# The first six expert matrices of a mixture of experts, loaded as halves into a pool that is then opened again

## The chip, the cores and the metric

The kernel runs on one core of one Trainium2 chip, as one program and one launch. The metric is the time of one execution on the device, in microseconds (us). TensorE is called PE below, VectorE DVE, ScalarE ACT, GpSimd POOL, and SyncE SP. SP issues every DMA of this kernel in the order of its own queue. Sizes of loads are in KB and MiB of 1024; rates are in GB/s of 10^9.

## The reference, cut to what matters

Two transformer blocks over 256 tokens of width 1024, all in fp32. The first block is a gated feed-forward layer, a recurrent mixer and a second gated feed-forward layer. The second block is an attention, a spatial gate, an output projection, and this mixture of experts, on which the change bears:

```python
for g in range(N_GROUPS):      # 4 groups of 8 experts, each expert 1024 x 512, 1024 x 512, 512 x 1024
    h = jax.nn.silu(jnp.einsum('nd,edf->nef', xt, w_gate[g])) * jnp.einsum('nd,edf->nef', xt, w_up[g])
    out = out + jnp.einsum('nef,efd->nd', h * combine[:, g, :, None], w_down[g])
```

Each token uses two experts of one group, but all 32 experts get tokens, so all 96 matrices of 2 MiB have to come out of HBM once: 192 MiB.

## The kernel before

The program runs through the first block, then through attention, gate and router of the second, and then through the experts. All weights ahead of the experts stream through SP into `wr` tiles of 1 MiB (line 118); ACT and DVE split each into a high part `whi` and a low part `wlo` for PE.

**The experts** run in 16 rounds `r`, two experts `e` = 0, 1 a round. A round needs three pairs of matrices `k`: gate (0), up (1), down (2). PE takes the pairs in the order (0,0), (0,1), (1,0), (1,1), (0,2), (2,0), (2,1), (1,2), (3,0) and so on, written (r,k): the down step of a round comes after gate and up of the next. `gate_up` (matmuls on line 1321) walks over j = 0..7 and takes e = 0 and e = 1 in turn at each j, so it reads the first half of both matrices at j = 0..3 and the second half of both at j = 4..7. In (0,0) the second half of `gather` stands between j = 3 and j = 4. `down` has its matmuls on line 1344. The matmuls and the small steps between them stand in an order written out by hand.

**Where the matrices lie.** A matrix is a tile `mw` of 16 KB on each of 128 partitions. There are 11 buffers. Six are the pool `mw1`, opened on the left side of SBUF at the end of the first block, so that its loads can start while attention still runs. Five are `mw2`, opened on the right side when attention is over and its buffers `wraw`, `whl`, `xgp` are given back. The matrices are numbered n = 0..95 in the order of use, and n takes buffer n mod 11: n = 0..5 are (0,0), (0,1), (1,0) in `mw1`, n = 6..10 lie in `mw2`, and n = 11, the second matrix of (2,0), is the first that goes back into a buffer of `mw1`, that of n = 0. It has one more place: its first half goes into `hx`, the 8 KB in which attention kept its result `h`, as soon as `h` is no longer needed.

```python
first = hx.tile([128, 2048], F32, name="hx")[:, :] if n_loads[0] == MW else None
t = whole_tile()
w.append([t[:, 0:2048] if first is None else first, t[:, 2048:4096]])
```

**What orders the loads.** Every load is issued by SP on line 1158. A load waits on SP until the last reader of what lay in its place is done, and the loads behind it in SP's queue wait with it. Up to the end of attention a scheduler decides how the loads of `wr` and of `mw` stand in that queue. Pools are opened with `reuse_waits="tile"`. The pool `mt2`, with the working tiles of the experts (`mxg`, `ms`, `hT`, `y`, ...), lies on the left in the place of attention's buffers.

Of the kernel before, what the change touches and what calls it, by code (L numbers as in the profile page):

```python
# [9 lines left out]
F32 = mybir.dt.float32  # L10
# [21 lines left out]
MW1 = 6  # L32
# [12 lines left out]
CUTS = ((0, 4096), (0, 2048, 4096), (0, 1024, 2048, 3072, 4096), (0, 1024, 2048, 3072, 3584, 4096))  # L45
# [28 lines left out]
def body(nc, tc, ap, dbg=None, stop=None):  # L74
    dbg = dbg or {}
    ctx = ExitStack()
# [6 lines left out]
    def pool(stack, name, bufs=1, space=None, side=None):  # L83
        kw = {"space": space} if space is not None else {}
        if side:
            kw["side"] = side
        return stack.enter_context(tc.tile_pool(name=name, bufs=bufs, reuse_waits="tile", **kw))
# [4 lines left out]
    with ctx:  # L92
# [87 lines left out]
        for q in range(4):  # L180
            r = slice(32 * q, 32 * q + 32)
# [43 lines left out]
        for q in range(4):  # L225
            r = slice(32 * q, 32 * q + 32)
# [136 lines left out]
        with ExitStack() as st:  # L363
            mp = pool(st, "mp")
            mt = pool(st, "mt", 2)
# [5 lines left out]
            parts = mp.tile([128, 2, 1024], F32R, name="parts")  # L371
# [72 lines left out]
            for base, src, dst, n in ((0, tw, sg, 0), (32, wa[32:64], ta, 4)):  # L444
                for h in range(2):
                    hs = slice(2 * h, 2 * h + 2)
                    ps = psR.tile([128, 2, T], F32, name="r")
                    for i in range(2):
                        p = 2 * h + i
                        TE.matmul(ps[:, i], lor[base:base + 32, p * 128:(p + 1) * 128], src, start=True, stop=True)  # L450
                    for i in range(2):
                        p = 2 * h + i
# [94 lines left out]
            for b in range(2):  # L547
                ms = [(i, c, 8 * i + 4 * b + c) for i in range(2) for c in range(4)]
                ps = psR.tile([128, 2, 4, C], F32, name="r")
                for i, c, m in ms:  # L550
                    for q in range(4):
                        r = slice(32 * q, 32 * q + 32)
# [3 lines left out]
                for i, c, m in ms:  # L556
                    for q in range(4):
                        r = slice(32 * q, 32 * q + 32)
                        TE.matmul(ps[r, i, c], NT[r, m], Yo[r, m], start=True, stop=True)
                for q in range(4):  # L560
                    r = slice(32 * q, 32 * q + 32)
# [38 lines left out]
            for s in range(2):  # L600
                r = sides[s]
# [14 lines left out]
            for c in range(NCH):  # L616
# [7 lines left out]
                if c < NCH - 1:  # L624
# [4 lines left out]
                    for s in range(2):  # L629
                        r = sides[s]  # L630
# [36 lines left out]
            for p in range(4):  # L667
                lerped(rr[:, p])
                for s in range(2):
                    r = sides[s]  # L670
# [158 lines left out]
            V.reciprocal(t[:, 1], t[:, 0])  # L829
            return t[:, 1]  # L830

        mw1 = pool(ctx, "mw1", MW1)
        hx = pool(ctx, "hx")
        hst = ctx.enter_context(ExitStack())
        hres = pool(hst, "hres")
        h = hx.tile([128, 2048], F32, name="hx").rearrange("p (a n) -> p a n", a=2)
# [6 lines left out]
        with ExitStack() as st:  # L843
# [134 lines left out]
            for i in range(4):  # L978
                q, k = following
# [154 lines left out]
        MW = MW1 + MW2  # L1134
        mw2 = [pool(ctx, f"mw2{i}", 1, side="right") for i in range(MW2)]
        rt = pool(ctx, "rt", side="right")
        n_loads = [0]

        def whole_tile():
            n = n_loads[0] % MW  # L1140
            p = mw1 if n < MW1 else mw2[n - MW1]
            n_loads[0] += 1
            return p.tile([128, 4096], F32, name="mw")

        def load(r, k):

            fine = 1 + k if r == 15 else int((r, k) == (14, 2))
            w, parts = [], []
            for e in range(2):
                first = hx.tile([128, 2048], F32, name="hx")[:, :] if n_loads[0] == MW else None  # L1150
                t = whole_tile()
                w.append([t[:, 0:2048] if first is None else first, t[:, 2048:4096]])
                cuts = CUTS[fine if first is None else 1]
                for s0, s1 in zip(cuts, cuts[1:]):
                    dst = t[:, s0:s1] if first is None or s0 else first
                    parts.append((s0, e, dst, ap["wm"][2 * r + e, k, :, s0:s1]))
            for s0, e, dst, src in sorted(parts, key=lambda x: x[:2]) if fine else parts:
                nc.sync.dma_start(dst, src)
            return w

        hnh = rt.tile([128, 2, D], F32R, name="hnh")
# [16 lines left out]
        with ExitStack() as st:  # L1178
# [15 lines left out]
            def small(name, k, n=None):  # L1194
                return rp.tile([128, k] + ([n] if n else []), F32, name=name)
# [51 lines left out]
            ex, w = small("ex", 8, 8), small("w", 6, 8)  # L1247
# [21 lines left out]


        with ExitStack() as st:
            mt = pool(st, "mt2", 1)
            psG = pool(st, "psG", 2, PSUM)
            psX = pool(st, "psX", 2, PSUM)
            def gather(g, steps=range(4), xg=None):
# [36 lines left out]
            def gate_up(r, k, mid=None):  # L1312

                w = load(r, k)
                ps = psG.tile([128, 512], F32, name="g")
                for j in range(NJ):
                    if mid and j == 4:
                        mid()
                    for e in range(2):
                        c = r % 2 * 128 + 64 * e  # L1320
                        TE.matmul(ps[64 * e:64 * e + 64], xg[:, j, c:c + 64],  # L1321
                                  w[e][j // 4][:, (j % 4) * 512:(j % 4) * 512 + 512], start=j == 0, stop=j == NJ - 1)
                return ps
# [11 lines left out]
            def down(r, hT, between=None):  # L1335

                wd = load(r, 2)
                pd = [psG.tile([128, 512], F32, name="g") for f in range(2)]
                ys = hx.tile([128, 2048], F32R, name="hx").rearrange("p (f n c) -> p f n c", n=2, f=2) if r == 15 else None
# [79 lines left out]
            tc.keep_in_program_order(S.preload_act_table_set("sqrt_and_others"))  # L1419


        fin = [mw1.tile([128, 4096], F32, name="mw") for n in range(2)]
        gfin, hsq, out = fin[0][:, 0:D], fin[1][:, 0:D], fin[1][:, 2048:4096].rearrange("p (a n) -> p a n", a=2)
        rowvec(gfin, "gfin")

# [23 lines left out]
        with tc.If(most > SLOT), ExitStack() as st:  # L1449
# [8 lines left out]
            with tc.For_i(0, NE, 1) as e:  # L1458
                w = []
# [7 lines left out]
                for n, src in enumerate((rk, comb)):  # L1467
                    m = ov.tile([128, 2, NE], F32, name="om")
# [135 lines left out]
```

## Time and profile before

| | |
|---|---|
| median of three runs | 1136.05 us (1135.2 to 1138.19) |
| the profiled execution's own time | 1135.7 us |
| its span, first to last instruction | 1134.0 us |
| around the span (launch, end) | 1.7 us |
| PE busy | 1079.0 us, 95% of the span |
| DVE, ACT, POOL busy | 538.7, 405.9, 139.5 us |
| moved by DMA | 304.69 MB, mean 269 GB/s |
| mean granted TensorE clock | 0.982 |

Busy time of PE is modelled from pipelined matmuls, so 95% does not say that PE sets the time of every stage. Shares over the whole span mix the first 680 us, where the weights move at some 180 GB/s, with the experts, where they move at 427 GB/s. The stages have to be read apart. The profiled execution is 0.35 us under the median of the three runs.

### The profile page before, as it was taken

What the parts mean: (1) busy time and instruction counts of PE and PEld (TensorE: products, weight loads), DVE (VectorE), ACT (ScalarE), POOL (GpSimd) and SP (SyncE); (2) the same over time, 40 slices, a digit from 0 to 9 for tenths busy, and PEclk for the clock granted to TensorE, in tenths of its full rate; (3) what the DMA queues carried; (4) which work ended last, traced back from release to release, by engine and by line L of the source; (5) the groups of instructions that cost most, each with busy time, mean ns of one, the idle gap of its engine ahead of it and who ended that gap; (6) DMA issues with size and microseconds to landing.
All of it is one profiled execution on the core that took longest, in us unless ns stands there. A gap on an engine that the chain in (4) does not pass through costs nothing.

```text
span 1134.0 us, 18469 instructions
## 1 busy us (share of the span) xinstructions
PE 1079.0 (95%) x7762; PEld 795.9 (70%) x7762; DVE 538.7 (48%) x966; ACT 405.9 (36%) x677; POOL 139.5 (12%) x139
## 2 busy tenths in 40 slices
PE   7999999868998999999999989999999999999996
PEld 6999999868788999999997864444344344534432
DVE  6766666799568766657655761211112121101112
ACT  5544454633544644445465631111011111101102
POOL 5000000663343200001134020000000000000000
PEclk9999999988998999999999999999999999999998
DMA  7655555422114555545677487999999999999994
GB/s 246 212 179 180 182 185 185 149 75 76 39 55 160 201 186 186 178 162 185 249 306 297 149 316 286 427 427 427 426 427 426 427 429 426 425 427 429 422 414 166
DMA packets 33319, 304.69 MB, mean 269 GB/s; under 512 B 4016, under 2 KB 4272, under 8 KB 9168
## 3 DMA queue, kind: packets, MB, share of 16 engines
q1 hardware_dynamic: 33232, 303.46, 67.8%
q8 instruction: 63, 1.03, 0.4%
q14 instruction: 24, 0.20, 0.1%
HBM read 302.40 MB, written 1.05 MB: 268 GB/s over the span
## 4 chain that ended last, share of the span: by engine, by line
PE 75%; DMA 14%; DVE 6%; ACT 2%; issue 1%; POOL 1%; SPq 0%; ACTq 0%; DVEq 0%; POOLq 0%
PE g L1321 14%; DMA mw<-wm 13%; PE gu L270 11%; PE gu L271 11%; PE gu L269 11%; PE g L1344 7%; PE u L269 3%; PE u L271 2%; PE u L270 2%; PE x L1286 2%; DVE wlo L261 1%; PE z L1375 1%; PE f L1375 1%; DMA wr<-w 1%; PE f L1006 1%
## 5 line engine op out<-in xcount | busy, mean ns | idle before, releaser
L261 DVE TENSOR_TENSOR wlo<-wr,whi 128x1024 fp32r<-128x1024 f32 (+3 forms) x182 | 202.7, 1119 | 93.9 <-ACT whi L260 92.8
L260 ACT CAST whi<-wr 128x1024 fp32r<-128x1024 f32 (+3 forms) x200 | 182.0, 918 | 168.0 <-PE gu L270 66.8
L1321 PE MATMUL g<-mw,mxg 128*64 128x512 f32 x1016 | 231.0, 595 | 1.2 <-DMA mw<-wm 1.2
L269 PE MATMUL gu<-xgh,whi 128*128 128x256 f32 x704 | 201.9, 287 | 6.8 <-ACT whi L260 6.8
L271 PE MATMUL gu<-xgh,wlo 128*128 128x256 f32 x704 | 201.4, 286 | 0.7 <-DVE wlo L261 0.7
L270 PE MATMUL gu<-xgl,whi 128*128 128x256 f32 x704 | 201.3, 286 | 0.5 <-DVE xgl L283 0.5
L1321 PEld LDWEIGHTS g<-mw,mxg 128*64 128x64 f32 x1016 | 76.0, 137 | 136.8 <-issue 129.3
L269 PEld LDWEIGHTS gu<-xgh,whi 128*128 128x128 f32 x704 | 137.0, 195 | 7.2 <-ACT whi L260 7.1
L271 PEld LDWEIGHTS gu<-xgh,wlo 128*128 128x128 f32 x704 | 136.9, 194 | 1.2 <-DVE wlo L261 1.2
L270 PEld LDWEIGHTS gu<-xgl,whi 128*128 128x128 f32 x704 | 137.0, 195 | 1.1 <-DVE xgl L283 1.0
L1344 PE MATMUL g<-mw,hT 128*64 128x512 f32 x512 | 121.1, 603 | 6.2 <-DMA mw<-wm 6.2
L269 PE MATMUL gu<-hh,whi 128*128 128x256 f32 x352 | 98.6, 280 | 0.0
L271 PE MATMUL gu<-hh,wlo 128*128 128x256 f32 x352 | 98.6, 280 | 0.0
L270 PE MATMUL gu<-hl,whi 128*128 128x256 f32 x352 | 98.0, 279 | 0.0
L1344 PEld LDWEIGHTS g<-mw,hT 128*64 128x64 f32 x512 | 39.9, 138 | 73.9 <-issue 59.1
L1350 ACT ACTIVATE y<-g,cs 128x512 fp32r<-128x512 f32 x30 | 20.6, 687 | 181.1 <-PE g L1344 120.5
L1351 DVE SCALAR_TENSOR_TENSOR y<-g,cs,y 128x512 fp32r<-128x512 f32 x30 | 22.5, 751 | 122.9 <-ACT y L1350 122.9
L269 PE MATMUL u<-xgh,whi 128*128 128x256 f32 x224 | 66.7, 298 | 1.7 <-DVE lb L434 1.2
L270 PE MATMUL u<-xgl,whi 128*128 128x256 f32 x224 | 65.6, 293 | 0.5 <-DVE xgl L283 0.5
L269 PEld LDWEIGHTS gu<-hh,whi 128*128 128x128 f32 x352 | 66.1, 188 | 0.0
L271 PEld LDWEIGHTS gu<-hh,wlo 128*128 128x128 f32 x352 | 66.1, 188 | 0.0
L270 PEld LDWEIGHTS gu<-hl,whi 128*128 128x128 f32 x352 | 66.0, 188 | 0.0
(473 smaller groups left out, 1564.2 us busy)
## 6 DMA issues: line engine op xcount, KB each, us to landing
mw<-wm SPq DMA_DIRECT2D x87, 2048.0 KB, 28.2
wr<-w SPq DMA_DIRECT2D x91, 1024.0 KB, 4.8
mw<-wm SPq DMA_DIRECT2D x9, 1024.0 KB, 15.1
mw<-wm SPq DMA_DIRECT2D x14, 512.0 KB, 15.0
xT<-xT SPq DMA_DIRECT2D x4, 256.0 KB, 5.0
wr<-w SPq DMA_DIRECT2D x4, 256.0 KB, 7.1
wr<-w SPq DMA_DIRECT2D x2, 512.0 KB, 7.3
hx<-wm SPq DMA_DIRECT2D x1, 1024.0 KB, 7.8
```

The costliest lines, as they stand in the source:

```text
L260: state["split"] = S.copy(hi[:, b], raw[:, b])
L261: (eng or V).tensor_tensor(lo[:, b], raw[:, b], f32(hi[:, b]), op=OP.subtract)
L269: TE.matmul(ps, wh, xh, start=i == 0, stop=False)
L270: TE.matmul(ps, wh, xl, start=False, stop=False)
L271: TE.matmul(ps, wl, xh, start=False, stop=i == n - 1)
L1006: TE.matmul(af[:, hp, :W], ntri, sp[:, hp], start=True, stop=False, skip_group_check=True)
L1286: last = TE.matmul(ps[:, i], x[:, a, j * 128:(j + 1) * 128], one[:, a], start=n == 0, stop=n == 3)
L1321: TE.matmul(ps[64 * e:64 * e + 64], xg[:, j, c:c + 64], w[e][j // 4][:, (j % 4) * 512:(j % 4) * 512 + 512], start=j == 0, stop=j == NJ - 1)
L1344: TE.matmul(pd[f][64 * e:64 * e + 64], hT[:, i, 64 * e:64 * e + 64], wd[e][i // 2][:, c:c + 512], start=i == 0, stop=i == 3)
L1350: S.activation(y[:, 0], pd[f], AF.Copy, scale=c)
L1351: V.scalar_tensor_tensor(y[:, 1], pd[f], c, f32(y[:, 0]), op0=OP.mult, op1=OP.subtract)
L1375: TE.matmul(acc[a][f], ct[:, r % 2, a], y[:, n], start=False, stop=False)
```

## The change

The pool `mw1` of six buffers of 16 KB is replaced at first by `mw0`, twelve buffers of 8 KB in 96 KB as before. The matrices n = 0..5 are loaded as twelve halves, for each pair first the first halves of e = 0 and e = 1, then the second halves. When the load of (2,0) is written, `mw0` is closed and `mw1` with six buffers of 16 KB is opened in its place, and n = 11, 12, ... go there as whole tiles. The 8 KB in `hx` now take the first half of n = 12 (the first up matrix of round 2), and n = 11 is loaded whole. So that `mw0` can be closed, `hx` is opened ahead of it, and `mt2` moves to the right side, behind `rt`.

```diff
-        mw1 = pool(ctx, "mw1", MW1)
         hx = pool(ctx, "hx")
+        mst = ctx.enter_context(ExitStack())
+        mw = [pool(mst, "mw0", 2 * MW1)]
...
+            if n < MW1:
+
+                for x in range(2):
+                    for e in range(2):
+                        w[e][x] = mw[0].tile([128, 2048], F32, name="mw")
+                        parts.append((2048 * x, e, k, w[e][x]))
+            else:
+                if n == MW - 1:
+                    mst.close()
+                    mw[0] = pool(mst, "mw1", MW1)
+                for e in range(2):
+                    if n + e == MW:
+                        early.append(hx.tile([128, 2048], F32, name="hx"))
+                        parts.append((0, 0, 1, early[0]))
+                    t = buffer(n + e)
+                    w[e] = [t[:, 0:2048], t[:, 2048:4096]]
+                    cuts = CUTS[fine]
+                    if n + e == MW + 1:
+                        w[e][0], cuts = early[0], (2048, 4096)
+                    parts += [(s0, e, k, t[:, s0:s1]) for s0, s1 in zip(cuts, cuts[1:])]
...
-            mt = pool(st, "mt2", 1)
+            mt = pool(st, "mt2", 1, side="right")
...
-        fin = [mw1.tile([128, 4096], F32, name="mw") for n in range(2)]
+        fin = [mw[0].tile([128, 4096], F32, name="mw") for n in range(2)]
```

**SP's queue during attention.** `wr` tiles are attention's weights, `mw` tiles of 128x4096 whole expert matrices, of 128x2048 halves. Before:

```order
L1158 DMA mw<-wm 128x4096
L118 DMA wr<-w 128x2048 x4
L1158 DMA mw<-wm 128x4096 x2
L118 DMA wr<-w 128x2048 x2
L1158 DMA mw<-wm 128x4096 x3
L118 DMA wr<-w 128x2048 x5
L1158 DMA mw<-wm 128x4096 x5
```

After the change, the same place:

```order
L1174 DMA mw<-wm 128x2048
L118 DMA wr<-w 128x2048
L1174 DMA mw<-wm 128x2048
L118 DMA wr<-w 128x2048 x3
L1174 DMA mw<-wm 128x2048 x3
L118 DMA wr<-w 128x2048
L1174 DMA mw<-wm 128x2048
L118 DMA wr<-w 128x2048
L1174 DMA mw<-wm 128x2048 x6
L118 DMA wr<-w 128x2048 x5
L1174 DMA mw<-wm 128x4096 x5
```

Six loads of 2 MiB have become twelve of 1 MiB, more finely mixed with the eleven loads of `wr`, whose own order is the same; the five `mw2` loads that follow are as they were.

**SP's queue at the end of attention**, with the semaphores on which each load waits (PE, DVE, Pool: the engine's own count; DMAHW: an earlier load). Before, from the last `mw2` load, n = 10, on; `mw_8222` is the second half of n = 11, and then come n = 12, 13, ...:

```order
L1158 DMA mw_8220<-wm 128x4096 [waits Pool_49]
L1158 DMA hx_8221<-wm 128x2048 [waits DVE_49,PE_49,Pool_49]
L1158 DMA mw_8222<-wm 128x2048 [waits PE_49]
L1158 DMA mw_8257<-wm 128x4096 [waits PE_49]
L1158 DMA mw_8258<-wm 128x4096 [waits DMAHW1_49,PE_49]
L1158 DMA mw_8280<-wm 128x4096 [waits DMAHW2_49,PE_49]
L1158 DMA mw_8281<-wm 128x4096 [waits DMAHW3_49,PE_49]
L1158 DMA mw_8312<-wm 128x4096 [waits DMAHW4_49,PE_49]
L1158 DMA mw_8313<-wm 128x4096 [waits DMAHW5_49,PE_49]
```

After the change; `mw_8238` is n = 11, `mw_8273` the second half of n = 12, and `mw_8274` to `mw_8328` are n = 13 to 16:

```order
L1174 DMA mw_8236<-wm 128x4096 [waits Pool_49]
L1174 DMA hx_8237<-wm 128x2048 [waits DVE_49,PE_49,Pool_49]
L1174 DMA mw_8238<-wm 128x4096 [waits PE_49]
L1174 DMA mw_8273<-wm 128x2048
L1174 DMA mw_8274<-wm 128x4096 [waits DMAHW7_49]
L1174 DMA mw_8296<-wm 128x4096 [waits DMAHW0_49]
L1174 DMA mw_8297<-wm 128x4096 [waits DMAHW1_49]
L1174 DMA mw_8328<-wm 128x4096 [waits DMAHW2_49]
L1174 DMA mw_8329<-wm 128x4096 [waits DMAHW3_49,PE_49]
```

Before, each load into a buffer of `mw1` has a wait for PE of its own. Now the first has one, the five behind it have none, and the next stands at `mw_8329`, n = 17, which goes into `mw2`.

## Rows read from the trace of the kernel before

**Rows 1.** The page: busy time of DMA engines and rate, 40 slices of the span

```profile
DMA  7655555422114555545677487999999999999994
GB/s 246 212 179 180 182 185 185 149 75 76 39 55 160 201 186 186 178 162 185 249 306 297 149 316 286 427 427 427 426 427 426 427 429 426 425 427 429 422 414 166
```

**Rows 2.** Stages of the experts: us, busy of engines (count), PE clock, DMA share, GB/s

```profile
681.30:693.60 12.30, 12.30 (x66) 7.14 (x67) 3.33 (x13) 3.17 (x5) 0.00 (x0) 0.90 0.44 186
693.60:707.30 13.70, 13.70 (x65) 4.41 (x62) 0.75 (x2) 0.60 (x1) 0.00 (x0) 1.00 0.93 353
707.30:720.00 12.70, 12.22 (x72) 6.68 (x74) 3.47 (x11) 1.82 (x4) 0.00 (x0) 1.00 1.00 427
720.00:1080.00 360.00, 353.55 (x1698) 153.04 (x1696) 58.47 (x122) 41.52 (x78) 0.00 (x0) 1.00 1.01 427
```

**Rows 3.** The chain that ended last, from 930 us: start, us, what

```profile
948.24 38.48 DMA mw<-wm
...
986.78 39.53 DMA mw<-wm
...
1036.19 39.16 DMA mw<-wm
1075.37 15.06 DMA mw<-wm
1090.45 15.08 DMA mw<-wm
...
1105.58 5.36 PE g L1344 x22
```

**Rows 4.** Waits of PE from 740 us on: us, times, longest

```profile
PE g L1344 <- DMA mw<-wm: 6.2, 3, 2.7
PE g L1321 <- DMA mw<-wm: 1.2, 2, 0.6
```

**Rows 5.** SP's issues from 681 us on: start, us, what

```profile
681.29 0.33 SPq L1158 DMA_DIRECT2D hx<-wm  x1
693.57 0.80 SPq L1158 DMA_DIRECT2D mw<-wm  x2
```

**Rows 6.** SP's issues at 707 us, and the first one's size and landing

```profile
707.30 0.81 SPq L1158 DMA_DIRECT2D mw<-wm  x2
...
mw<-wm SPq DMA_DIRECT2D x1, 2048.0 KB, 12.6
```

**Rows 7.** SP's waits from 676 to 740 us: us in total, times, longest

```profile
SPq L1158 <- PE g L1321: 40.5, 5, 12.0
```

**Rows 8.** The chain from 680 to 740 us: start, us, what

```profile
684.26 3.58 PE g L1321 x16
687.85 2.11 PE x L1286 x16
689.96 17.32 PE g L1321 x80
707.27 0.60 PE x L1329 x4
...
710.31 7.02 PE g L1321 x32
...
729.83 7.02 PE g L1321 x32
```

**Rows 9.** Windows of 2 us around the issue at 693.57, columns as in rows 2

```profile
692.00:694.00 2.00, 2.00 (x12) 0.72 (x10) 0.00 (x0) 0.39 (x1) 0.00 (x0) 1.00 0.00 0
694.00:696.00 2.00, 2.00 (x12) 0.63 (x10) 0.00 (x0) 0.21 (x1) 0.00 (x0) 1.00 0.74 180
696.00:698.00 2.00, 2.00 (x12) 0.67 (x10) 0.00 (x0) 0.00 (x0) 0.00 (x0) 1.00 1.04 434
```

**Rows 10.** The load issued at 558.35 us, alone on the engines: size, us to landing

```profile
mw<-wm SPq DMA_DIRECT2D x1, 2048.0 KB, 7.7
```

**Rows 11.** Attention, and a stretch of loads of 1 MiB and less, columns as in rows 2

```profile
558.00:600.00 42.00, 40.75 (x278) 35.76 (x276) 24.40 (x38) 26.04 (x37) 12.24 (x10) 1.00 0.77 307
600.00:640.00 40.00, 38.65 (x243) 32.01 (x242) 22.81 (x31) 24.86 (x40) 10.10 (x13) 1.00 0.67 261
1080.00:1100.00 20.00, 20.00 (x98) 8.30 (x96) 2.93 (x6) 2.25 (x4) 0.00 (x0) 1.00 1.02 414
```

**Rows 12.** Tile wr, 555 to 652 us: what ended idle time before its readers; landing

```profile
  ACT whi L260: 14.6, 6
...
  ACT catb L948: 0.4, 1
...
DMA to landing us min/median/max: 4.7/4.9/6.9
```

More of the change, by code (lines that the diff above doesn't have):

```diff
@@ L1136, in body, with buffer @@
         rt = pool(ctx, "rt", side="right")
[L1137 to L1142, printed above, removed]
+        n_loads, early = [0], []
+        def buffer(n):
+            p = mw[0] if n % MW < MW1 else mw2[n % MW - MW1]
             return p.tile([128, 4096], F32, name="mw")
         def load(r, k):
+            n = n_loads[0]
+            n_loads[0] += 2
             fine = 1 + k if r == 15 else int((r, k) == (14, 2))
[L1148 to L1158, printed above, removed]
@@ new lines, in load @@
+            w = [[None, None], [None, None]]
+            parts = []
+            if n < MW1:
[17 more added lines that the diff above has]
+                    parts += [(s0, e, k, t[:, s0:s1]) for s0, s1 in zip(cuts, cuts[1:])]
+                if fine:
+                    parts.sort(key=lambda x: x[:2])
@@ L1159, in load @@
+            for s0, e, m, dst in parts:
+                nc.sync.dma_start(dst, ap["wm"][2 * r + e, m, :, s0:s0 + dst.shape[1]])
             return w
```

## The prediction

> **What bounds the kernel now.** I read the page's slices first, to find the stage with its own limit. From slice 26 (709 us) to slice 37 the DMA engines are busy without a break at 425 to 429 GB/s [rows 1]; ahead of it the rate is uneven, and slice 25 (680 to 709 us) has only 286. So the experts are a stream of loads that runs at one rate, once it runs. The stages show the same: 427 GB/s from 707.3 to 1080 us, but 186 and 353 in the two stretches before, while PE is busy through both [rows 2]. The chain that ended last says what sets the end: from 948.2 us it consists of loads alone, apart from two short stretches of PE, until the load that lands at 1105.5 releases the last matmuls [rows 3]. PE waits for weights only 7.4 us in all from 740 us on [rows 4]: it starts with eleven matrices in store and uses up that lead slowly, and by the end it has none left. The stream of loads therefore sets the end, and since it has no pause after 707 us, a pause ahead of that can't be won back, nor can a longer one.
>
> Next, what starts the stream. SP issues the load into `hx` at 681.29, and after it nothing until 693.57 [rows 5]; the waits of SP say what for, PE's matmuls of line 1321, longest 12.0 us [rows 7]. In the chain, the first 16 records of line 1321 at 684.26 are j = 0..3 of (0,0) (two records a matmul), then comes the gather, and the 80 records from 689.96 to 707.27 are the other 16 of (0,0), 32 of (0,1) and 32 of (1,0) [rows 8]. At 17.32 / 80 = 0.2165 us a record, (0,0) ends at 693.4, (0,1) at 700.4 and (1,0) at 707.3. So the load at 693.57 is the one that waited for buffer 0 of `mw1`, which (0,0) had just read to its end, and the two at 707.30 are those that waited for (1,0) [rows 5, 6, 8].
>
> **The change, part by part.**
>
> *The reopened pool.* This is the term that decides. The order shows the load of n = 11 with a wait for PE, and the loads of n = 12 to 16 with none. The new buffers 1 to 5 lie over the old halves of (0,0), (0,1) and (1,0): buffer 5, where n = 16 goes, covers the first and second place of the last four halves, those of (1,0). Since its load may not run before (1,0) is done and has no wait for PE of its own, the wait of n = 11 must already cover (1,0). The count that it waits for in the built program is indeed that of the last matmul of (1,0). All of `mw0` has to be free before the first whole tile may go there. So n = 11 is issued at 707.3, where before SP issued its second half at 693.57, and everything behind it in SP's queue waits as long: 13.7 us of late issue.
>
> What that costs the stream I work out in two ways. By bytes: before, 693.6 to 707.3 moved 353 x 13.7 = 4836 kB [rows 2], which at 427 GB/s is 11.3 us that now have to be run later. In addition the restart has a lag: after the issue at 693.57 the window up to 696 has 180 GB/s, against 434 in the next, so data flowed for 0.83 us of it and began at 695.2, 1.6 us after the issue [rows 9]. Before, no such lag followed 707.3; now one does. 11.3 + 1.6 = 12.9 us. By landings: before, the load issued at 707.30 landed 12.6 us later, at 719.9 [rows 6], the ninth MiB after `hx` (1 + 2 + 2 + 2 + 2). Now a first load of 2 MiB alone on the engines lands after 7.7 us [rows 10], the other 7 MiB behind it take 1.049 MB / 427 GB/s = 2.46 us each, 17.2: the ninth MiB lands at 707.3 + 24.9 = 732.2, 12.3 us later. I take the middle, 12.6. The bounds are 11.3 (no lag) and 13.7 (late issue, no credit).
>
> *Does the stream then run on?* At 707.3 SP issues n = 11 to 16 one behind the other, 11 MiB or 27 us of data. n = 17 goes into the buffer of n = 6, which (1,1) frees at 717.3 [rows 8], long before that runs out. So the stream is fed from 709 us on, as before. PE is not held up at once: (2,0) starts at 729.83 [rows 8], and n = 11 lands at 707.3 + 7.7 = 715. PE simply has 12.6 us less lead and runs out of it earlier; its waits for weights grow from 7.4 [rows 4] to about 20 us.
>
> *The halves.* They can free the first places earlier: the first halves of (0,0) are read to their end at 687.85, 5.7 us before the whole tile was released. But nothing may use that place before 707.3, so this is worth nothing. Loading them in halves costs attention little. The same 12 MiB go through 558 to 640 us, where DMA's share is 0.77 and 0.67, so of 82 us some 23 are free [rows 11]. Loads of 1 MiB and less run at 414 GB/s where whole ones run at 427 [rows 2, 11]: 12.6 MB / 414 - 12.6 / 427 = 0.9 us, in that free time. Six more issues of 0.33 us (that of `hx`, rows 5) fall where SP has nothing else. The `wr` loads take 4.7 to 6.9 us to land, the late ones behind 2 MiB of experts; of the ten rows of what ended idle time before their readers none is a load [rows 12]. They will come up to 2.5 us earlier, with 1 MiB less ahead of them, and nobody waits for them. I take 0, with 0.5 either way for what the scheduler shifts.
>
> The page "DMA: Bandwidth & Descriptors" of the Trainium skill (section "Bandwidth") speaks against the halves: it tells to batch transfers, and has 341 GB/s for one of 1 MB where one of 16 MB gets 425. By that, as an estimate from the page, the twelve halves would take 12.6 MB / 341 - 12.6 MB / 425 = 7.3 us more of the DMA engines, and if all of it fell on attention the sum would be 1155.8 us. This trace does not agree: loads of 1 MiB and less that stand one behind the other in the queue ran at 414 GB/s [rows 11].
>
> *`hx` and `mt2`.* The 1 MiB in `hx` goes out at the same 681.29 and is only another half matrix. `mt2` on the right takes the place of the router's small tiles; PE's order there is the same and the first `gate_up` follows its gather without a gap (684.26, rows 8). I take 0.
>
> *Sum.* Against the profiled execution: span 1134.0 + 12.6 = 1146.6, with the 1.7 us around it 1148.3 us. The median of the three runs is 0.35 us above the profiled execution: 1136.05 + 12.6 = 1148.65. I predict 1148.5 us, slower by 1.1%.
>
> **The rivals.**
>
> *The places are released one by one.* If n = 11 may go as soon as its own two halves are read, it is issued at 687.9, n = 12's second half at 693.6, n = 13 after four j of (0,1) at 697, then 700.4, 704 and 707.3. With the 1.6 us of lag and 2.46 us a MiB, the eleventh MiB after `hx` lands about 719.5, where before it landed one load of 4.9 us behind 719.9, at 724.8. The kernel would take 1136.05 - 5.3 = 1130.7 us. For it: before, each load waits for its own reader. Against it: the five loads without a wait for PE. 4%.
>
> *Nothing happens, because PE sets the end.* For it: PE is busy 95%, and waits for weights only 7.4 us [rows 4]. If the late stream still reached PE in time, it would be 1136. Against: the chain of loads from 948 us and 427 GB/s to the end [rows 2, 3]; there is no slack to take 12 us. 3%.
>
> *The halves hold up attention as well.* Each load could bring the lag of an issue into an idle queue, 1.6 us [rows 9], and the `wr` loads behind it as much: six added loads, 9.6 us, if PE then waits for its weights, which gives 1158. It decides from the point where a `wr` load lands after its buffer's turn comes. Against: the loads queue behind each other, where rows 11 show no lag, and nobody waits for `wr` [rows 12]. 4%. The page's rule above is a milder form of it.
>
> **How the numbers follow.** 89% for the forecast, whose own range is 1147.3 to 1149.8 by the bounds 11.3 and 13.7, and with the runs' scatter of 1 to 2 us and the 0.5 of attention 1145 to 1151. 4, 3 and 4% for the rivals. The range that I give, 1144.5 to 1151, leaves out the three rivals and little else. A change within 0.3% (3.4 us) can't be told from none here. Slower by more than that: 0.93 (forecast and third rival). Within it: 0.03. Faster: 0.04 (the first rival).
>
> **What would show it.** SP idle from the issue of `hx` near 681 to 707, then six loads of line 1174 in one row; DMA at 0 GB/s from 688 to 708.9, where before it was 0 only to 695; the ninth MiB at 732; 427 GB/s from 709 on and the last load 12 to 13 us later than before; PE's waits for `mw` near 20 us; everything ahead of 681 us within 0.5 us of before. I am wrong if the load after `hx` goes out before 700 us (the first rival), if the stream has further pauses after 709, or if the experts start at another time than 684.

## The result and the profile after

The changed kernel takes 1148.32 us (median of four runs, 1144.8 to 1150.51), the kernel before beside it 1135.62 us: a ratio of 1.0114, 95% interval [1.0096, 1.0131], or 12.7 us slower. 1148.5 was predicted, from a loss of 12.6 us.

The profiled execution took 1144.8 us, with a span of 1143.1. It is the shortest of the four. It came to the experts earlier than the kernel before did in its own profile: (0,0) starts at 680.37, there at 684.26 [rows 8]. From there to the end of the span it needs 1143.1 - 680.4 = 462.7 us, before 1134.0 - 684.3 = 449.7: the experts lost 13.0 us.

The page of after, the DMA rows of its 40 slices and the shares of the chain that ended last, in which the loads have 31%, where before they had 14%:

```profile
DMA  7655555322124555555686483999999999999994
GB/s 259 210 185 185 184 182 178 120 75 76 44 86 171 189 185 184 185 177 183 241 334 263 166 332 137 428 428 424 428 427 427 428 425 429 427 426 429 423 414 170
PE 56%; DMA 31%; DVE 7%; ACT 2%; issue 1%; POOL 1%; SPq 0%; ACTq 0%; DVEq 0%; POOLq 0%
```

The slice that had 286 GB/s before [rows 1] has 137, and from the next on the rates are those of before. What was lost was lost in one place. SP's issues there (start, us, what), and after them SP's waits from 676 to 740 us (in total, times, longest):

```profile
677.22 0.33 SPq L1174 DMA_DIRECT2D hx<-wm  x1
703.42 10.84 SPq L1174 DMA_DIRECT2D mw<-wm  x8
```

```profile
SPq L1174 <- PE g L1337: 40.2, 3, 25.9
```

After `hx` SP issues nothing for 26 us, held by PE's matmuls of line 1337 in one wait of 25.9, where before the longest was 12.0 and there were five [rows 7]. The chain from 680 us (start, us, what) tells whose end it waited for:

```profile
680.37 3.58 PE g L1337 x16
683.95 2.11 PE x L1302 x16
686.06 17.32 PE g L1337 x80
703.38 0.60 PE x L1345 x4
```

(1,0) ends at 703.38, and n = 11 is issued at 703.42. The stages (us, busy of engines with counts, PE clock, DMA share, GB/s) show the pause and the restart:

```profile
688.00:694.00 6.00, 6.00 (x30) 2.01 (x28) 0.00 (x0) 1.88 (x2) 0.00 (x0) 1.00 0.00 0
694.00:705.00 11.00, 10.52 (x53) 3.84 (x50) 1.34 (x4) 0.87 (x2) 0.00 (x0) 1.00 0.10 18
705.00:709.00 4.00, 4.00 (x26) 2.25 (x28) 1.60 (x6) 0.00 (x0) 0.00 (x0) 1.00 0.89 360
709.00:720.00 11.00, 11.00 (x62) 5.25 (x59) 1.78 (x5) 1.64 (x3) 0.00 (x0) 1.00 1.01 427
720.00:1080.00 360.00, 350.13 (x1659) 155.66 (x1659) 57.17 (x119) 40.85 (x77) 0.00 (x0) 1.00 1.01 427
```

No byte moves from 688 to 694 and hardly one up to 705, and from 709 on the stream runs at the 427 GB/s that it had before [rows 2]. The landings of n = 11, issued at 703.42, and of n = 15, issued at 705.32 (KB, us from issue to landing):

```profile
mw<-wm SPq DMA_DIRECT2D x1, 2048.0 KB, 8.9
mw<-wm SPq DMA_DIRECT2D x1, 2048.0 KB, 24.2
```

n = 15 completes the ninth MiB after `hx` (2 + 1 + 2 + 2 + 2), at 729.5, or 49.1 us after (0,0) began. Before, the ninth MiB landed at 719.9 [rows 6], 35.7 us after it. PE's waits for weights from 740 us on grew from 7.4 [rows 4] to 14.5:

```profile
PE g L1360 <- DMA mw<-wm: 12.4, 6, 2.7
PE g L1337 <- DMA mw<-wm: 2.1, 4, 0.6
```

So the size and the place are as predicted. But why n = 11 waits for (1,0) was only argued, and the experiments had to test that.

### The profile page after: what moved, and what is told of

Read it like the earlier page. It is cut to its first block, busy times and chain, and to the rows that moved or that the text cites. A ratio compares the mean times of both kernels' runs of the same rounds, so it can differ in the third digit from the quotient of the medians.

```text
span 1143.1 us, 18471 instructions
## 1 busy us (share of the span) xinstructions
PE 1077.8 (94%) x7762; PEld 795.2 (70%) x7762; DVE 538.8 (47%) x966; ACT 405.9 (36%) x677; POOL 139.0 (12%) x139
## 4 chain that ended last, share of the span: by engine, by line
PE 56%; DMA 31%; DVE 7%; ACT 2%; issue 1%; POOL 1%; SPq 0%; ACTq 0%; DVEq 0%; POOLq 0%
DMA mw<-wm 30%; PE gu L271 11%; PE gu L269 11%; PE gu L270 11%; PE g L1337 5%; PE g L1360 2%; PE u L269 2%; PE u L271 2%; PE u L270 2%; DVE wlo L261 1%; PE x L1302 1%; DMA wr<-w 1%; DVE big L436 1%; ACT whi L260 1%; PE f L1007 1%
## 5 line engine op out<-in xcount | busy, mean ns | idle before, releaser
L1337 PE MATMUL g<-mw,mxg 128*64 128x512 f32 x1016 | 233.9, 595 | 2.1 <-DMA mw<-wm 2.1
L1337 PEld LDWEIGHTS g<-mw,mxg 128*64 128x64 f32 x1016 | 80.1, 137 | 133.9 <-issue 119.0
L1360 PE MATMUL g<-mw,hT 128*64 128x512 f32 x512 | 125.6, 604 | 12.4 <-DMA mw<-wm 12.4
L271 PE MATMUL u<-xgh,wlo 128*128 128x256 f32 x224 | 66.0, 294 | 0.0
```

Of the source, the lines that this page charges most:

```text
L271: TE.matmul(ps, wl, xh, start=False, stop=i == n - 1)
L1337: TE.matmul(ps[64 * e:64 * e + 64], xg[:, j, c:c + 64], w[e][j // 4][:, (j % 4) * 512:(j % 4) * 512 + 512], start=j == 0, stop=j == NJ - 1)
L1360: TE.matmul(pd[f][64 * e:64 * e + 64], hT[:, i, 64 * e:64 * e + 64], wd[e][i // 2][:, c:c + 512], start=i == 0, stop=i == 3)
```

## The experiments

Ratios are to the kernel before, run on the same chip, with 95% intervals.

**Only the reopening, only a part of it.** The first kernel keeps whole matrices in `mw0` and still closes it and opens `mw1`. The other two load in halves only the first load, (0,0), or the first two, (0,0) and (0,1), in a pool `mw0` of their own that is then reopened; the remaining buffers of 16 KB are in `mwk`, which stays.

The first edit is that of whole matrices, the second that of one load in halves (with two, `MWH` is 4):

```diff
-        mw = [pool(mst, "mw0", 2 * MW1)]
+        mw = [pool(mst, "mw0", MW1)]
...
-                for x in range(2):
-                    for e in range(2):
-                        w[e][x] = mw[0].tile([128, 2048], F32, name="mw")
-                        parts.append((2048 * x, e, k, w[e][x]))
+                for e in range(2):
+                    t = mw[0].tile([128, 4096], F32, name="mw")
+                    w[e] = [t[:, 0:2048], t[:, 2048:4096]]
+                    parts.append((0, e, k, t))
```

```diff
+        MWH = 2
+        mwk = pool(ctx, "mwk", MW1 - MWH)
...
-        mw = [pool(mst, "mw0", 2 * MW1)]
+        mw = [pool(mst, "mw0", 2 * MWH)]
...
-            p = mw[0] if n % MW < MW1 else mw2[n % MW - MW1]
+            p = mw[0] if n % MW < MWH else mwk if n % MW < MW1 else mw2[n % MW - MW1]
...
-            if n < MW1:
+            if n < MWH:
...
-                    mw[0] = pool(mst, "mw1", MW1)
+                    mw[0] = pool(mst, "mw1", MWH)
```

> Everything of the change but the halves: the pool is closed and opened again at the same place, with six whole buffers both times; hx ahead of it and mt2 on the right as in the change. In the built program n = 11 now waits for (0,0) alone, and n = 12 to 16 have waits of their own again. Theory (the wait for the whole old pool, which comes with the change of buffer size, costs the 12.6 us): the load behind hx goes out when (0,0) ends, some 12 us after hx, and the time is that of before, 1135.6 us, within 2 us. Rival (reopening as such, or mt2 on the right, or hx for n = 12, costs): 1142 to 1148 us.

> The change for the first pair alone: (0,0) in four halves in the pool that is opened again with two whole buffers; (0,1) and (1,0) whole in a pool of four that stays open. The wait of n = 11 must then cover (0,0) only, which is what its second half waited for before. Theory: the load goes out some 12 us after hx, 1135.6 us within 2 us. Rival (the halves or a reopened pool cost something by themselves): above 1139 us.

> The change for the first two pairs: (0,0) and (0,1) in eight halves, reopened as four whole buffers; (1,0) whole in a pool of two that stays open. n = 11 then waits for the end of (0,1), 6.9 us after that of (0,0) and 6.9 us ahead of that of (1,0). Theory: half of the loss. Before, 693.6 to 700.4 moved some 2.3 MB, 5.3 us at 427 GB/s, and 1.6 us of lag come on top, less 1 us of a dip at 702 to 706 that no longer occurs: 5.9 us, 1141.5 us, range 1139.5 to 1143.5. Rival (the loss does not depend on which reader is waited for): 1148 us, or 1135.6.

Measured: 1135.6 us, 0.9996 [0.9985, 1.0008], for whole matrices; 1134.55 us, 0.9996 [0.9985, 1.0007], for one load in halves; 1142.32 us, 1.0055 [1.0041, 1.0069], for two. SP's waits from 676 to 740 us, with one load in halves, and then with two:

```profile
SPq L1176 <- PE g L1339: 41.1, 5, 12.5
```

```profile
SPq L1176 <- PE g L1339: 40.7, 4, 19.3
```

The longest wait grows with the part that is loaded in halves, 12.5, 19.3, 25.9 us: up to the end of (0,0), of (0,1), of (1,0). Closing and opening a pool costs nothing by itself, nor does `mt2` on the right or `hx` taking n = 12, which the kernel with whole matrices has too. All three came out as expected. But whether n = 11, where sizes differ, waits for the whole old pool or only for the last half loaded into it, they can't tell: in the two with halves both are free at the same moment.

**One tile in place of the reopened pool.** The six buffers become one tile of 96 KB that is never released, and halves and whole matrices are slices of it, buffer b over halves 2b and 2b+1. Each load then waits for the readers of its own slice.

```diff
-        mw = [pool(mst, "mw0", 2 * MW1)]
+        big = pool(mst, "mw0").tile([128, 4096 * MW1], F32, name="mw")
...
+            c = n % MW
+            if c < MW1:
+                return big[:, 4096 * c:4096 * c + 4096]
...
-                        w[e][x] = mw[0].tile([128, 2048], F32, name="mw")
+                        c = 4096 * n + 4096 * x + 2048 * e
+                        w[e][x] = big[:, c:c + 2048]
...
-                if n == MW - 1:
-                    mst.close()
-                    mw[0] = pool(mst, "mw1", MW1)
...
```

> The halves kept, the reopening taken away: the six buffers are one tile of 96 KB that is never given back, cut by hand, with the same places as in the change (buffer b over the halves 2b and 2b+1). Each load then waits for the last reader of its own place: n = 11 for j = 3 of (0,0), n = 12 for the end of (0,0), n = 13 for j = 3 of (0,1) and so on. Theory: the load behind hx goes out some 6 us after hx; eleven MiB after hx are there 5 to 6 us earlier than before: 1130 us, range 1128 to 1132.5. Rival (the end is not set by the stream, or the halves hold up attention): 1135 us or more.

Measured: 1134.22 us, 0.9988 [0.9975, 1.0000], and in a second measurement 1134.89 us, 0.9994 [0.9984, 1.0005]. A miss: the loss is gone, but of the 5 us of gain there is about 1. The loads themselves went out as expected. SP's waits from 676 to 740 us, and windows of 12 us from 36 us after the issue of `hx` on:

```profile
SPq L1173 <- PE g L1336: 41.3, 8, 9.7
```

```profile
715.29:727.29 12.00, 12.00 (x69) 6.06 (x65) 3.44 (x7) 2.59 (x5) 0.00 (x0) 1.00 0.96 396
727.29:739.29 12.00, 12.00 (x58) 4.86 (x58) 1.18 (x2) 1.56 (x3) 0.00 (x0) 1.00 0.96 382
739.29:751.29 12.00, 12.00 (x58) 4.02 (x53) 1.50 (x3) 0.69 (x1) 0.00 (x0) 1.00 1.01 433
```

Eight waits, none over 9.7 us, and yet 396 and 382 GB/s where the kernel before ran at 427 [rows 2]. The pair of loads behind the wait of down(0) says why: it was issued at 727.38, in the kernel before at 728.72 in its own span (KB, us from issue to landing; first one tile, then before):

```profile
mw<-wm SPq DMA_DIRECT2D x1, 2048.0 KB, 8.5
```

```profile
mw<-wm SPq DMA_DIRECT2D x1, 2048.0 KB, 10.8
```

8.5 us is little over the 7.7 of a load alone on the engines [rows 10]: the queue had all but run dry, because this load waits for a buffer that down(0) has to give back, however early the loads ahead of it went. Counted from the issue of `hx`, the 11th MiB landed 3.4 us earlier than before (40.2 against 43.5), the 17th only 1.7 earlier (727.38 + 8.5 - 679.29 = 56.6 against 728.72 + 10.8 - 681.29 = 58.2). The stream gave half of its lead back at the next buffer that PE had not yet read (in the profile of the second measurement 4.7 us became 2.1).

**down(0) earlier.** To test that, the same kernel with down(0) ahead of both parts of the second `gather` in round 1, so that the buffer comes free earlier.

```diff
-                    if r % 2 and r < 15:
+                    if r % 2 and 1 < r < 15:
                         gn = r // 2 + 1
...
                         y = down(r - 1, hT, rest)
+                    if r == 1:
+                        xn = gather(1, range(4), mt.tile([128, NJ, 256], F32, name="mxg"))
```

> e4 with one step of PE moved: in round 1 the down step of round 0 stands ahead of both parts of the gather for rounds 2 and 3, not around them. In e4 the stream ran dry again at 728 us, because n = 19 and 20 wait for the places of the down matrices, which PE gives back at 727.4; the two parts of the gather ahead of that take 2.1 us each. Theory (e4 gave its gain back at that point): those loads go out 4.2 us earlier, the pause of 1.7 us at 728 to 730 is gone, and the time is 1.5 to 3 us under that of e4: 1132 us, range 1130.5 to 1134. Rival (the gain of e4 was lost elsewhere, or PE sets the end): no difference to e4.

Measured: 1131.88 us, 0.9968 [0.9957, 0.9979]. The pair is issued at 724.25, and lands with other loads still ahead of it:

```profile
mw<-wm SPq DMA_DIRECT2D x1, 2048.0 KB, 12.0
```

The 17th MiB lands 724.25 + 12.0 - 681.47 = 54.8 us after `hx`, 3.4 us ahead of before, where the kernel with one tile was 1.7 ahead, and this shows in the time (1135.4 x 0.0032 = 3.6 us). So the place of down(0) is what cost that kernel half of its lead. Not all of the lead is kept here either: the 11th MiB landed 39.0 us after `hx`, 4.6 us ahead of before, and some 1 us of that is gone by the 17th.

**Halves for longer, reopened later.** If a pool reopened with another size waits for all of the old one, the stall should move with the reopening. Both kernels go on loading the left side in halves, up to n = 65 or up to n = 21, and reopen it with the next matrix; the edit is that of the first, the other has 22.

```diff
+        REOPEN = 66
...
+            if n == REOPEN:
+                mst.close()
+                mw[0] = pool(mst, "mw1", MW1)
+            halved = [m % MW < MW1 and m < REOPEN for m in (n, n + 1)]
...
-                if n == MW - 1:
-                    mst.close()
-                    mw[0] = pool(mst, "mw1", MW1)
...
```

> The change with the reopening moved: the six places are used as twelve halves up to n = 65, and the pool is closed and opened with whole buffers at n = 66. That load still waits for all of the old pool (the reader of n = 60). In e4 that reader was done at 955.3 us while the load ahead of n = 66 landed at 962.9, so the wait ends 5 us (after 1.6 us of lag) before the queue is empty. Theory (a wait costs only as much as the queue runs dry): no pause there; 1134.2 us of e4 plus the price of some thirty matrices in loads of 1 MiB, about 0.08 us each, 2.4 us: 1136.6, range 1134 to 1139. Rival (closing and reopening with another size costs 12 us wherever it stands): 1147 us.

> The same with the reopening at n = 22, early, where the queue is short. n = 22 then waits for the reader of n = 16, the end of (3,0), at 759.1 us in e4, while the load ahead of it landed at 745.6 there. Theory: SP's queue is dry from about 745 to 759.1 + 1.6; pause 15 us; with 0.5 us for six matrices as halves 1149.7 us, range 1147 to 1152.5. Rival (a fixed price of the reopening, 12 us on e4): 1146.5 us; or none, 1135.

Measured: 1134.36 us, 0.9993 [0.9981, 1.0004], with the reopening at 66, and 1132.98 us, 0.9982 [0.9972, 0.9991], with that at 22. The first lies in its range. The second was to lose 14 us and lost nothing. By the theory its load of n = 22 had to wait for the end of (3,0), which reads n = 16. SP's issues of n = 22 and of n = 27, the load into the place of n = 16, and PE's matmuls of (3,0) (start, us, what):

```profile
733.61 0.42 SPq L1181 DMA_DIRECT2D mw<-wm  x1
756.74 0.33 SPq L1181 DMA_DIRECT2D mw<-wm  x1
749.70 7.02 PE g L1344 x32
```

n = 22 goes out 16 us before (3,0) even begins, and only n = 27 waits for its end. The stretch from 740 to 1060 us of this kernel, and that of the kernel with 66 (columns as in the windows above):

```profile
740.00:1060.00 320.00, 317.29 (x1541) 134.33 (x1538) 54.37 (x114) 38.34 (x72) 0.00 (x0) 0.99 1.01 427
```

```profile
740.00:1060.00 320.00, 316.70 (x1534) 135.35 (x1532) 53.95 (x113) 37.51 (x70) 0.00 (x0) 0.99 1.01 424
```

No pause in 320 us of either. So a reopened pool does not wait for all of the old one, and the theory of the prediction had fallen.

**Where the tiles lie.** I then read the addresses in the built program of the changed kernel, in KB from the pool's start, in the order of first use:

```
halves of mw0   0: 0   1: 88   2: 80   3: 72   4: 64   5: 56   6: 48   7: 40   8: 32   9: 24   10: 16   11: 8
buffers of mw1  n=11: 0-16   n=12: 80-96   n=13: 64-80   n=14: 48-64   n=15: 32-48   n=16: 16-32
```

The first tile lies at the start, the second at the top, and the others follow downward. So n = 11 lies over half 0, the first of (0,0), and over half 11, which is the last of (1,0). n = 12 lies over halves 1 and 2, n = 13 over 3 and 4, and so on up to n = 16 over 9 and 10. All of these are free earlier (half 10 by one matmul only, the others by 3 us and more), but their loads stand behind n = 11 in SP's queue. That explains the wait with a release tile by tile. It explains the kernel that reopens at 22 as well: its second pass has only eleven halves, since the first half of n = 12 is in `hx`, so nothing new lies at 8 to 16 KB.

**One load at another place in the order.** If that is right, it is enough that a half of (0,0) is loaded last. Two kernels issue all twelve half loads in one go at n = 0. In the first, the second half loaded (e = 1, j = 0 to 3 of (0,0)) comes last; in the second, a control, `q` runs over `range(12)`, the order of the changed kernel. In both, the third load takes its data from (0,2) in place of (1,0), as many bytes from another place.

```diff
+                if n == 0:
+                    for q in (0, *range(2, 12), 1):
+                        p, x, e = q // 4, q // 2 % 2, q % 2
+                        halves[q] = mw[0].tile([128, 2048], F32, name="mw")
...
+                w = [[halves[2 * n + 2 * x + e] for x in range(2)] for e in range(2)]
```

> The changed kernel with its twelve half loads issued in one go at the first of them, and the second half of (0,0)'s first places (expert 1, places j = 0 to 3) issued last of the twelve instead of second. So the reopened pool's buffer 0 lies over the two halves that the first four places of (0,0) read, and buffers 1 to 5 over the halves read next, two by two. Theory A (a buffer of the reopened pool waits only for the tiles that lay at its own addresses; in the changed kernel buffer 0 lay over the first half loaded and over the last one, which (1,0) reads, and SP's queue held the five loads behind it): the load n = 11 goes out about 6 us after hx instead of 26, the six loads go out some 3.4 us apart, and the time is that of the kernel with one tile cut by hand, 1134.5 us (1132.5 to 1136.5). Theory B (my prediction's: all of the old pool must be free before the first whole tile): the load still waits for the end of (1,0), and the time stays 1148 us (1146 to 1150).

> Control to the kernel in which one half is loaded last: the twelve half loads are issued in one go too, but in the changed kernel's own order, so that buffer 0 lies over the first half and over the last half of (1,0). It differs from the other kernel in the place of one load among twelve alone. Both theories: n = 11 waits for the end of (1,0), 26 us, and the time is that of the changed kernel, 1148 us (1146 to 1150). If it came out near 1135, issuing the twelve in one go would have been what helps, and neither theory would be told apart.

Measured: 1133.76 us, 0.9979 [0.9969, 0.9988], with one half last, and 1147.86 us, 1.0117 [1.0102, 1.0132], for the control. SP's waits from 676 to 740 us and the issues after `hx`, first with one half last:

```profile
SPq L1176 <- PE g L1339: 40.6, 8, 9.7
```

```profile
682.78 0.33 SPq L1176 DMA_DIRECT2D hx<-wm  x1
689.37 0.33 SPq L1176 DMA_DIRECT2D mw<-wm  x1
695.05 0.33 SPq L1176 DMA_DIRECT2D mw<-wm  x1
```

and the control:

```profile
SPq L1176 <- PE g L1339: 40.4, 3, 26.0
```

```profile
679.37 0.33 SPq L1176 DMA_DIRECT2D hx<-wm  x1
705.74 38.88 SPq L1176 DMA_DIRECT2D mw<-wm  x14
```

6.6 us after `hx` against 26.4. The place of one load among twelve is worth 14 us: the wait is that of one buffer on one late half. The built programs say the same: with one half last, each of the loads of n = 11 to 16 waits for PE, each for a later count than the one ahead of it; in the control, as in the changed kernel, of these six only n = 11 does, for the last matmul of (1,0). The pause is in the windows of 12 us from 12 us after the issue of `hx` on, first with one half last, then the control:

```profile
694.78:706.78 12.00, 12.00 (x58) 4.02 (x56) 0.75 (x2) 1.88 (x2) 0.00 (x0) 1.00 0.97 365
```

```profile
691.37:703.37 12.00, 12.00 (x58) 4.02 (x56) 0.75 (x2) 1.88 (x2) 0.00 (x0) 1.00 0.00 0
```

**The same with (1,0)'s own data, and with down(0) earlier.** The third load's halves come from (1,0) again; the second kernel has the edit of round 1 from above as well.

```diff
-                        p, x, e = q // 4, q // 2 % 2, q % 2
+                        x, e, (r0, k0) = q // 2 % 2, q % 2, ((0, 0), (0, 1), (1, 0))[q // 4]
```

> The kernel in which one half is loaded last of the twelve, with the third load's four halves taken from (1,0) as in the changed kernel (in the two runs before they were taken from (0,2), the same amount of data). Data do not enter any of the theories: 1133.8 us (1132.5 to 1135.5), a ratio of 0.998 to the kernel before. Were it nearer 1148, the time of the run with (0,2) would have had another reason than buffer 0's place.

> The same, and in round 1 down(0) ahead of both gather parts, the edit that gave the kernel with one tile cut by hand 2.5 us. Theory A (the place of buffer 0 is the whole loss, and the gain of the earlier release is limited by the stream running dry again at 728 us, while PE is in gather): 1131.5 us (1130 to 1133). If the reopened pool cost anything of its own besides, it would stay 1 us or more above the kernel with one tile, which gave 1131.9.

Measured: 1133.7 us, 0.9981 [0.9966, 0.9997], and 1131.83 us, 0.9964 [0.9952, 0.9976]. Both as expected. A reopened pool costs no more than one tile cut by hand, once its first buffer lies over halves that are free early. These two, the kernel with one tile and down(0) earlier, and that with the reopening at 22 are faster than the kernel before, by 0.2 to 0.4%.

## Why the prediction was right, and where its reason was wrong

- **The sum.** 12.6 us were predicted, 12.7 measured, and 13.0 in the profile from (0,0) to the end. The ninth MiB landed 49.1 us after (0,0) began, where 732.2 - 684.3 = 47.9 was predicted. The 1.2 us are those by which the first load landed later than a load alone, 8.9 against 7.7 [rows 10]. The lag of 1.6 us is one in effect: the first packets moved 1.0 us after the issue, before (693.57) as after (703.42), and the full rate came later.
- **The reopened pool: the right wait for a wrong reason.** The step that failed is "All of `mw0` has to be free before the first whole tile may go there". I had the count on which n = 11 waits, that of (1,0), and five loads without a wait behind it, and took that for a rule of the pool. In its place the runs showed that a buffer waits for what lay at its own addresses (the reopening at 22, and the pair that differs by the order of loads). The buffers were also taken to lie one after the other, with n = 16 over the late halves; n = 16 does lie over two of the late ones (9 and 10), but it is n = 11 that lies over the last. The five loads had no wait because SP's queue had waited for them already. That both reasons give the same wait here is luck of the layout: with one half loaded last, the same kernel does not lose anything (1133.7 us), and the prediction's reason would have called for 1148 there too.
- **The stream runs on.** Right: 427 GB/s from 709 us on.
- **PE's waits.** About 20 us were predicted, 14.5 came. The stall was taken to be idle time only: from (0,0) to the end PE's busy time grew too, from 431.3 to 437.1 us, with 2069 and 2068 records. 7.1 + 5.8 make 12.9 of the 13.0. The growth sits in the matmuls that read the experts' weights (count, busy us, mean ns of one, idle before; first before, then after):

```profile
L1321 PE MATMUL g<-mw,mxg 128*64 128x512 f32 x1016 | 231.0, 595 | 1.2 <-DMA mw<-wm 1.2
L1344 PE MATMUL g<-mw,hT 128*64 128x512 f32 x512 | 121.1, 603 | 6.2 <-DMA mw<-wm 6.2
L1337 PE MATMUL g<-mw,mxg 128*64 128x512 f32 x1016 | 233.9, 595 | 2.1 <-DMA mw<-wm 2.1
L1360 PE MATMUL g<-mw,hT 128*64 128x512 f32 x512 | 125.6, 604 | 12.4 <-DMA mw<-wm 12.4
```

As many of the same mean length cover more time, so they overlap less. That this happens where they come one by one behind late weights was not tested.
- **The halves.** Nearly right: the price of 0 in attention was not measured by itself, but no run shows one. In a long queue halves cost a little. Beside the kernel that reopens at 22, the one that reopens at 66 has 48 more loads of 1 MiB in place of 24 of 2 MiB; it takes 1.4 us more (1134.36 against 1132.98 us on the same chip), and its stream runs at 424 in place of 427 GB/s. Against the kernel before it has 70 more. By the rule of the Trainium skill that was weighed in the prediction ("DMA: Bandwidth & Descriptors", section "Bandwidth"; its figures are of transfers issued from GpSimd, and these loads are issued by SP), 73.4 MB at 341 in place of 425 GB/s would be 43 us more, as an estimate from the page. The measurement disagrees: with 12 of every 22 MiB in loads of 1 MiB the stream ran at 424 GB/s beside 427. Wrong was "nothing may use that place before 707.3": with one half last it is used 6.6 us after `hx`.
- **`hx` and `mt2`.** Right, by the kernel with whole matrices.
- **Ahead of 681 us.** "Within 0.5 us" was too much to ask of two executions: (0,0) starts at 680.4 after, 684.3 before, and between 680.6 and 686.5 in the profiles of the other kernels. That goes with TensorE's granted clock (third number from the end) from 200 to 400 us, first before, then after:

```profile
200.00:400.00 200.00, 178.47 (x2083) 163.25 (x2082) 155.57 (x298) 102.02 (x196) 82.09 (x67) 0.94 0.31 108
200.00:400.00 200.00, 176.60 (x2096) 161.42 (x2095) 156.90 (x301) 102.42 (x197) 80.48 (x63) 0.96 0.31 109
```

In that stretch the clock falls from 2.4 to 1.2 GHz for some us at a time; before, PE was busy 4.8 of the 10 us from 220 on, and in the next 10 us the granted clock was 0.67. Of 14 profiles the five with 0.96 reach (0,0) at 680.3 to 683.0, the four with 0.94 at 684.2 to 686.4; the kernel before, with whole matrices, is at the early end of these four, and the other three have halves. So the start says little on the change, and the sign of being wrong "if the experts start at another time than 684" was a poor one; profiles are better compared from (0,0) on.
- **The rivals.** *Places released one by one* had 4%. As a mechanism it is what happens, with n = 11 over a late half, which the rival had over two early ones. Where it does lie over early ones, the price was still wrong: with one tile the lead is 3.4 and 4.7 us in two profiles, not 5.3, and half of it is given back where down(0) holds the next buffer. That PE sets the end fell with the result; that the halves hold up attention, with the kernels in halves that lose nothing.

## What to carry to other kernels

Before a pool is reopened with another tile size, look up which old tiles each new buffer lies over: loads wait in the order of the queue, and one new buffer over a late tile holds all of them. A wait count shows what is waited for, not which rule made it, so test the rule with a case in which two rules differ. Loads that go out earlier win only as far as the next buffer that the reading engine has not given back; moving that step forward was worth 2 to 3 us more, at least as much as the release itself.

## What the runs showed of the hardware

A load of 2 MiB that starts a dry stream landed after 7.6 to 7.8 us where it was alone or had one to three loads close behind it, and after 8.9 and 8.8 us where five more were issued behind it within 2.5 us (the changed kernel and the control); what makes the difference was not tried. A long queue in which 12 of every 22 MiB go as loads of 1 MiB up to n = 65, the rest as loads of 2 MiB, ran at 424 GB/s from 740 to 1060 us; with loads of 2 MiB it ran at 427.
